# First layer's second and third set of modulations: from TensorE in the projections to POOL and one-column products in attention

## The chip, the cores and the metric

The kernel runs on one core of one Trainium2 chip. The metric is the device time of one execution in microseconds. The core has five engines that work side by side: TensorE (PE; its weight loads are listed as PEld), VectorE (DVE), ScalarE (ACT), POOL (GpSimd) and SyncE (SP), which here only issues DMAs. Each engine works through its own queue in order; semaphores make it wait for others.

## The reference, cut to what matters

Two layers over 1024 latent tokens and 256 context tokens of width 1024. Every layer is steered by six vectors ("modulations") for the latents and six for the context, each a product of an activated conditioning vector with a 1024 x 6144 matrix. The first layer's mixer is attention beside a convolution:

```python
sc = jax.nn.silu(c)
scc = jax.nn.silu(c_ctx)
for l in range(DEPTH):
    mod_l = jnp.split((sc @ ada_w[l] + ada_b[l])[:, None, :], 6, axis=-1)
    mod_c = jnp.split(scc @ ada_w[l] + ada_b[l], 6, axis=-1)
    h_lat = rms_norm(x, norm1_g[l]) * (1 + mod_l[1]) + mod_l[0]
    h_ctx = rms_norm(ctx, norm1_g[l]) * (1 + mod_c[1]) + mod_c[0]
    ...                                   # l == 0: even_mixer, attention | convolution
    x = x + mod_l[2] * y_lat
    h = rms_norm(x, norm2_g[l]) * (1 + mod_l[4]) + mod_l[3]
    x = x + mod_l[5] * conv_ffn(h, ...)
    ...                                   # the same for ctx with mod_c
```

So modulations 0 and 1 are needed before the first projections, and 2 to 5 only after the mixer.

## The kernel before

Activations lie with channels on partitions and tokens along the free dimension: 8 tiles of 128 x 1280, context first. All large products are made of three products of rounded parts (`mm3`, lines 336 to 340): a number is split into a high and a low part, and high x high, high x low and low x high are summed. Weights come in units of 128 x 1024 (`wunit`): SyncE loads them, ScalarE rounds the high part, POOL subtracts for the low part (line 332).

The order of each engine's instructions is set when the kernel is built: the program is traced in the order of the Python code, and a planner with its own estimate of times then orders each engine's queue, taking what is ready first and, among that, what was traced first. The context manager `later(400)` makes what is traced inside it count as traced 400 instructions later. Tiles with one `tag` share `bufs` buffers. A `Side` is a list of generators whose pieces of work are traced between the steps of the main work: `run(us)` adds to an account, and each piece takes from it what it yields.

The work around the change, all in the first layer (`layer0`):

- *Start.* The sums of squares of x, and the first set of modulations (`ada_set` for set 0; a set is two modulations, 2048 columns). `ada_gen` loads the weights in tiles, 128 rows by 512 or 1024 columns, and TensorE multiplies them, in plain float32: the 128 x 32 tile `sc` (both conditioning vectors and 30 columns of zeros) stands still and 512 columns of weights stream through (line 365, tile `adaps`). The trace shows each such product as two records. ScalarE copies the result, TensorE turns it (line 374, `adapt`), VectorE adds the bias into `modT` (line 379).
- *Projections.* Four channel blocks of the convolution's gated input (`l0_conv`: two dense products each, tiles `dc` and `dl`, then VectorE multiplies by ScalarE's sigmoid), and five blocks of queries, keys and values (`l0_block`: per 128 tokens a 128 x 256 result `qkv` or `qkl`; ScalarE squares and copies it into `z`, VectorE and POOL normalize and rotate it, SyncE stores it). Between them a `Side` traces the depthwise convolution with 31 taps (`conv_taps`): 22 taps (30 in the last block) are VectorE's multiply-adds (`self.stt`, line 1162), the other 8 are multiplied by ScalarE (line 692, tile `ctap`, three buffers) and summed by DMAs that POOL issues with accumulation (line 693). The weights of modulation sets 1 and 2 are loaded here too, in the three `ctap` buffers, with `later(400)`.
- *Attention* (`attention_all`). Four groups of three heads; units of 256 queries, 12 long ones over 1280 keys and 3 short ones over 256 context keys in each group. Steps of scores and of values are interleaved by due times: 9 steps for a long unit and 3 for a short one, 468 in all. TensorE makes scores `S`, VectorE the maximum (line 995), ScalarE the exponential (line 996), TensorE turns the result (line 1018, tile `pT`, tag `pt`, two buffers), ScalarE and VectorE split it into `ph` and `pl` (lines 1022, 1023), TensorE multiplies by the values (line 1029), and SyncE stores the output to DRAM tiles `od` (line 1041). After each step `side.run(0.14)` traces a piece of the preparation of the next group (`stack_gen`, tiles `zst` on POOL and ScalarE, turned by TensorE, line 963), and `more.run(0.22)` a piece of the convolution's layer norm (`l0_ln`) and then of `load_early`: finished chunks of the mixer's output are read back from `od` and split by POOL into two parts (lines 800 to 804).
- *Output projection.* Ten chunks of 128 channels, in the order 6, 7, 8, 9 (convolution), 0 to 5 (heads): seven were split during attention, the last three are loaded and split afterwards by ScalarE and VectorE (`load_split`, lines 502 and 503), beside the loads of x. Here modulation 2 is used first.

The sums of squares in `ss_finish` (line 418) are one-column products: a 128 x 128 block of squares stands still and one column of ones streams through, which sums over partitions.

## Time and profile before

| | |
|---|---|
| median of 3 runs | 3935.66 us (3933.4 to 3939.22) |
| profiled execution | 3939.62 us, span 3937.4 us |
| mean granted TensorE clock | 0.962 |
| busy share of the span | TensorE 92%, weight loads 74%, VectorE 55%, ScalarE 32%, POOL 34% |

The numbers of the trace below are times of one execution, counted from the first instruction. The rows that name a line, an engine and tiles give what the group wrote, an arrow, and what it read; `x128` is the number of records. A row of a stretch gives for each engine its busy time and the number of records, then the granted TensorE clock, the busy share of the 16 DMA engines and GB/s. A row of a wait gives who waited, for whom, the total in us, how often, and the longest. A row of the timeline gives start and length in us, and in brackets the idle time before it with what ended it.

### The profile page before, as it was taken

What the parts mean: (1) busy time and instruction counts of PE and PEld (TensorE: products, weight loads), DVE (VectorE), ACT (ScalarE), POOL (GpSimd) and SP (SyncE); (2) the same over time, 40 slices, a digit from 0 to 9 for tenths busy, and PEclk for the clock granted to TensorE, in tenths of its full rate; (3) what the DMA queues carried; (4) which work ended last, traced back from release to release, by engine and by line L of the source; (5) the groups of instructions that cost most, each with busy time, mean ns of one, the idle gap of its engine ahead of it and who ended that gap; (6) DMA issues with size and microseconds to landing.
All of it is one profiled execution on the core that took longest, in us unless ns stands there. A gap on an engine that the chain in (4) does not pass through costs nothing.

```text
span 3937.4 us, 47862 instructions
## 1 busy us (share of the span) xinstructions
PE 3610.4 (92%) x18784; PEld 2923.8 (74%) x18784; DVE 2173.8 (55%) x2720; ACT 1251.1 (32%) x2126; POOL 1328.3 (34%) x1003
## 2 busy tenths in 40 slices
PE   7987688888899999999999899999976899999998
PEld 4767567767785558888888788988765778888886
DVE  5976366667223235554554579645598554343435
ACT  4135566666232112222222332322211342222222
POOL 3258331100251112332221445445466652222123
PEclk9999789999999999999999999999988999999999
DMA  5476111000323331222111257622245421111111
GB/s 200 121 187 149 44 57 31 21 24 19 108 78 110 110 106 61 66 75 70 60 59 38 75 173 215 185 95 91 97 155 198 134 69 43 50 42 54 43 54 54
DMA packets 204016, 356.38 MB, mean 91 GB/s; under 512 B 23632, under 2 KB 124560, under 8 KB 203792
## 3 DMA queue, kind: packets, MB, share of 16 engines
q1 hardware_dynamic: 172240, 311.22, 24.2%
q0 software_dynamic: 27648, 35.76, 4.3%
q10 hardware_dynamic: 3904, 6.36, 0.5%
q8 instruction: 148, 2.42, 0.3%
q14 instruction: 76, 0.62, 0.0%
HBM read 275.04 MB, written 62.39 MB: 86 GB/s over the span
## 4 chain that ended last, share of the span: by engine, by line
PE 68%; DVE 11%; issue 4%; ACT 3%; DMA 2%; POOL 2%; SPq 0%; POOLq 0%; ACTq 0%; DVEq 0%
PE dl L338 13%; PE dl L339 13%; PE dl L340 13%; PE adaps L365 2%; PE pj L338 2%; PE pj L339 2%; PE pj L340 2%; PE pT L1018 2%; PE o L1029 2%; DVE nm L995 2%; DVE pl L1023 2%; PE dc L340 2%; PE dc L339 2%; PE dc L338 1%; PE S L978 1%
## 5 line engine op out<-in xcount | busy, mean ns | idle before, releaser
L332 POOL TENSOR_TENSOR wlo<-wraw,whi 128x1024 fp32r<-128x1024 f32 (+1 forms) x226 | 560.6, 2486 | 1366.5 <-ACT whi L331 1266.5
L339 PE MATMUL dl<-hl,whi 128*128 128x512 f32 x1920 | 764.5, 398 | 4.2 <-POOL hl L1158 2.8
L338 PE MATMUL dl<-hh,whi 128*128 128x512 f32 x1536 | 608.6, 397 | 5.1 <-ACT nt L456 3.2
L340 PE MATMUL dl<-hh,wlo 128*128 128x512 f32 x1536 | 609.3, 397 | 0.0
L331 ACT CAST whi<-wraw 128x1024 fp32r<-128x1024 f32 (+1 forms) x226 | 224.8, 1005 | 917.3 <-PE dl L339 421.2
L339 PEld LDWEIGHTS dl<-hl,whi 128*128 128x128 f32 x1920 | 362.7, 189 | 99.0 <-issue 11.7
L1067 DVE SCALAR_TENSOR_TENSOR fc<-dl,cols,fc 128x1023 f32<-128x1023 f32 x84 | 107.6, 1281 | 548.6 <-ACT fc L1066 548.6
L338 PEld LDWEIGHTS dl<-hh,whi 128*128 128x128 f32 x1536 | 289.2, 188 | 86.8 <-issue 14.2
L340 PEld LDWEIGHTS dl<-hh,wlo 128*128 128x128 f32 x1536 | 289.5, 188 | 77.5 <-issue 10.1
L842 DVE SCALAR_TENSOR_TENSOR x<-dl,modT,x 128x1024 f32<-128x1024 f32 x160 | 204.7, 1280 | 164.2 <-PE dl L340 162.7
L338 PE MATMUL dl<-gs,whi 128*128 128x512 f32 x640 | 252.9, 395 | 5.1 <-DVE fc L1069 5.1
L339 PE MATMUL dl<-gs,whi 128*128 128x512 f32 x640 | 251.6, 393 | 0.0
L340 PE MATMUL dl<-gs,wlo 128*128 128x512 f32 x640 | 250.5, 391 | 0.0
L1018 PE MATMUL pT<-ident,p 128*128 128x128 f32 x1008 | 170.0, 292 | 40.6 <-DVE pl L1023 33.7
L1023 DVE TENSOR_TENSOR pl<-pT,ph 128x512 fp32r<-128x512 f32 x252 | 167.6, 686 | 66.3 <-ACT ph L1022 65.6
L1022 ACT CAST ph<-pT 128x512 fp32r<-128x512 f32 x252 | 142.7, 587 | 157.6 <-PE pT L1018 156.3
L995 DVE TENSOR_REDUCE nm<-S 128x1 f32<-128x1280 f32 (+1 forms) x120 | 153.0, 1275 | 55.5 <-PE S L979 51.5
L1029 PE MATMUL o<-ph,vs 128*128 128x256 f32 x504 | 146.5, 304 | 34.4 <-ACT ph L1022 17.4
L1018 PEld LDWEIGHTS pT<-ident,p 128*128 128x128 f32 x1008 | 124.3, 149 | 63.2 <-DVE pl L1023 47.3
L1162 DVE SCALAR_TENSOR_TENSOR conv<-u,cols,conv 128x1287 f32<-128x1287 f32 (+14 forms) x96 | 160.8, 1705 | 0.9
L365 PE MATMUL adaps<-adaw,sc 128*32 128x512 f32 x384 | 150.3, 621 | 7.8 <-DMA adaw<-in_adaw 7.4
L338 PE MATMUL dl<-hl,whi 128*128 128x512 f32 x384 | 154.9, 405 | 1.4 <-ACT whi L331 0.8
(368 smaller groups left out, 8351.8 us busy)
## 6 DMA issues: line engine op xcount, KB each, us to landing
wraw<-in_wup SPq DMA_DIRECT2D x88, 512.0 KB, 3.5
adaw<-in_adaw SPq DMA_DIRECT2D x128, 256.0 KB, 2.6
wraw<-in_wdn SPq DMA_DIRECT2D x44, 512.0 KB, 3.5
adaw<-in_adaw SPq DMA_DIRECT2D x32, 512.0 KB, 4.4
df<-in_dftf POOLq DMA_DIRECT2D x64, 256.0 KB, 4.2
wraw<-in_w1f SPq DMA_DIRECT2D x24, 512.0 KB, 3.6
x<-in_xT SPq DMA_DIRECT2D x16, 640.0 KB, 9.3
spd<-so SPq DMA_DIRECT2D x68, 128.0 KB, 2.7
```

Source lines behind the costliest of these rows:

```text
L331: nc.scalar.copy(hi[:, :cols], raw[:, :cols])
L332: nc.gpsimd.tensor_tensor(out=lo[:, :cols], in0=raw[:, :cols], in1=hi[:, :cols].bitcast(F32), op=ALU.subtract)
L338: mm(out, lhsT=lh, rhs=rh, start=first, stop=False)
L339: mm(out, lhsT=lh, rhs=rl, start=False, stop=False)
L340: mm(out, lhsT=ll, rhs=rh, start=False, stop=last)
L365: nc.tensor.matmul(ps[32 * i:32 * i + 32, :], lhsT=self.sc[:, k, :], rhs=w[:, b:b + 512], start=(k == 0), stop=(k == KD - 1), tile_positio ...
L842: nc.vector.scalar_tensor_tensor(out=xl, in0=pl, scalar=self.mod(l, j, m, 0), in1=xl, op0=ALU.mult, op1=ALU.add)
L995: nc.vector.tensor_reduce(out=nm[:, i:i + 1], in_=s, op=ALU.max, axis=AX.X, negate=True)
L1018: nc.tensor.transpose(pt[:, (2 * a + i) * P:(2 * a + i + 1) * P], p[:, kc * P:(kc + 1) * P], self.ident)
L1023: nc.vector.tensor_tensor(out=pl, in0=pt, in1=ph.bitcast(F32), op=ALU.subtract)
L1029: nc.tensor.matmul(o, lhsT=vs[:, kc], rhs=x[:, a * 256:a * 256 + 256], start=(kc == 0 and j == 0), stop=(kc == nk // P - 1 and j == 1))
L1162: self.nc.vector.scalar_tensor_tensor(out=out, in0=a, scalar=s, in1=b, op0=ALU.mult, op1=op)
```

## The change

Modulation sets 1 and 2 of the first layer are no longer formed by `ada_set` in the projections. A new generator, `ada_vec`, forms them during attention, as a third list of side work (`slow`, `slow.run(0.25)` after each step, a piece of 1.4 for each weight tile). For each set and each quarter of 512 columns it loads 8 weight tiles of 128 x 512; for both conditioning vectors POOL multiplies the tile by that vector's column (one number per partition) and adds the product to an accumulator of 128 x 512. Then TensorE sums over the partitions with one-column products, four blocks for each vector, into a PSUM tile `adv` with the tag `pt`, and VectorE adds the bias. The buffers for this (two each for weights, accumulators and products, 2 KB per partition each) lie in attention's pool; for them the mixer's chunks that are split during attention are six instead of seven, and `load_split` brings four afterwards instead of three.

```diff
+    def ada_vec(self, l, s, cs, wbuf, acc, psf, pool=None):
+        nc = self.nc
+        bias = self.col(f"adab{l}", 48, 2)
+        for j in range(4):
+            a = [acc(i) for i in range(len(cs))]
+            for k in range(KD):
+                w = wbuf()
+                nc.sync.dma_start(out=w, in_=self.i["adaw"][l, s, k, j // 2][:, j % 2 * 512:j % 2 * 512 + 512])
+                for i, c in enumerate(cs):
+                    f = self.sc[:, k, c:c + 1]
+                    if k == 0 or pool:
+                        t = pool() if k else a[i]
+                        (nc.gpsimd if pool else nc.vector).tensor_scalar(out=t, in0=w, scalar1=f, scalar2=None, op0=ALU.mult)
+                        if k:
+                            self.add(a[i], a[i], t, pool=True)
+                    else:
+                        self.stt(a[i], w, f, a[i])
+                yield 0.7 * len(cs)
+            ps = psf("adv")
+            n = len(cs)
+            for b in range(4):
+                for i in range(n):
+                    nc.tensor.matmul(ps[:, b * n + i:b * n + i + 1], lhsT=a[i][:, b * P:(b + 1) * P],
+                                     rhs=self.ones[:, 0:1], start=True, stop=True)
+            m = slice(s * 16 + 4 * j, s * 16 + 4 * j + 4)
+            self.add(self.modT[l][:, m, cs[0]:cs[-1] + 1], ps[:, :4 * n].rearrange("p (b c) -> p b c", c=n),
+                     bias[:, m, cs[0]:cs[-1] + 1])
...
-            ada = [(0, 1), (0, 2)]
...
-                if ada and (blk, c) in self.ADA:
-                    with self.later(400):
-                        self.ada_set(*ada.pop(0), lambda: c2.tile([P, UL], F32, name="adaw", tag="ctap", bufs=3), self.a_ps)
...
-            hs = early + self.load_split(oh, [self.od[k] for k in order[7:]], T, (512, TC + 512, T), 2)
+            hs = early + self.load_split(oh, [self.od[k] for k in order[6:]], T, (512, TC + 512, T), 2)
...
-    ADA = ((None, 0), (None, 1))
...
+        slow = Side()
+        for n in (1, 2):
+            slow.add(self.ada_vec(0, n, (0, 1), lambda: ab.tile([P, 512], F32, name="adaw", tag="adaw", bufs=2),
+                                  lambda i: ab.tile([P, 512], F32, name="adacc", tag="adacc", bufs=2),
+                                  lambda name: self.pa.tile([P, 512], F32, name=name, tag="pt", bufs=self.npt),
+                                  lambda: ab.tile([P, 512], F32, name="adap", tag="adap", bufs=2)))
...
-                        early = self.two_parts(7, "oc", self.oc)
+                        early = self.two_parts(6, "oc", self.oc)
...
-                                                  for c in {3: (0,), 5: (1, 2), 7: ()}[g]]))
+                                                  for c in {3: (0,), 5: (1,), 7: ()}[g]]))
...
             more.run(self.MORE)
+            slow.run(self.SLOW)
         more.drain()
+        slow.drain()
...
-    LEAD, SIDE, MORE = 1.35, 0.14, 0.22
+    LEAD, SIDE, MORE, SLOW = 1.35, 0.14, 0.22, 0.25
```

## The prediction

> **What bounds the kernel now.** I read the page first, for the share of TensorE and for the rows of the products that the change removes; then busy time by stretch, for the two stages that it touches; then the waits, the timeline and single tiles inside them.
>
> ```profile
> span 3937.4 us, 47862 instructions
> PE 3610.4 (92%) x18784; PEld 2923.8 (74%) x18784; DVE 2173.8 (55%) x2720; ACT 1251.1 (32%) x2126; POOL 1328.3 (34%) x1003
> L365 PE MATMUL adaps<-adaw,sc 128*32 128x512 f32 x384 | 150.3, 621 | 7.8 <-DMA adaw<-in_adaw 7.4
> ```
>
> TensorE is busy for 92% of the span, so work taken from it counts unless another engine is as full in that stage. The 384 records are six sets (two records to a product); the change takes two of them, 128 records. They lie in the projections (94 to 387 us); attention runs from 420 to 1007.
>
> ```profile
> core 0: us, PE busy (x) PEld busy (x) DVE busy (x) ACT busy (x) POOL busy (x), PEclk, DMA share, GB/s
> 94.00:387.00 293.00, 267.97 (x1726) 221.11 (x1724) 233.24 (x315) 100.03 (x414) 149.18 (x113) 0.98 0.58 149
> 420.00:1007.00 587.00, 474.33 (x2968) 397.39 (x2968) 380.05 (x576) 361.69 (x661) 93.16 (x167) 0.92 0.10 30
> 753.80:877.40 123.60, 102.80 (x680) 87.14 (x680) 84.63 (x128) 77.04 (x147) 7.99 (x19) 0.97 0.06 17
> 893.30:1007.20 113.90, 91.60 (x598) 77.13 (x596) 79.02 (x120) 65.50 (x117) 0.00 (x0) 0.97 0.04 9
> ```
>
> The projections are bound by TensorE (268 of 293 us) with VectorE close behind (233). Attention is a tight loop through TensorE, ScalarE and VectorE, TensorE 81% busy, POOL only 16%. The last two rows are the same stretch of head group 2 and of group 3, from the first of 15 stores of head outputs to the last (11 long units, 3 short), as in the row
>
> ```profile
> 893.35 114.28 SPq L1041 DMA_DIRECT2D od<-ot  x15
> ```
>
> I use them below.
>
> **The change part by part.**
>
> *Products out of the projections.* Busy time of this tile alone in the stage, one block of the timeline, and the waits:
>
> ```profile
> 94.00:387.00 293.00, 36.62 (x128) 4.94 (x128) 1.13 (x2) 0.98 0.58 149
> ...
> 153.62 0.28 PE L339 MATMUL qkv<-wlo,hh 128*128 128x256 f32 x1
> 153.74 0.28 PE L340 MATMUL qkv<-whi,hl 128*128 128x256 f32 x1
> 153.94 1.05 PE L365 MATMUL adaps<-adaw,sc 128*32 128x512 f32 x4
> 154.93 0.38 PE L338 MATMUL qkv<-whi,hh 128*128 128x256 f32 x1
> 155.15 0.28 PE L339 MATMUL qkv<-wlo,hh 128*128 128x256 f32 x1
> ...
> DVE conv L1158 <- DMA acc<-ctap: 23.5, 3, 14.6
> PE qkl L338 <- ACT z L751: 10.8, 6, 2.7
> DVE modT L379 <- PE adapt L374: 8.3, 1, 8.3
> PE adaps L365 <- DMA adaw<-in_adaw: 7.4, 3, 5.0
> ```
>
> Four records take 153.74 to 155.15, where two of the steps before (0.12 us) would have stood: 1.17 us each, and 32 such blocks are 37.4 us. TensorE waited 7.4 us more for their weights. The eight turns (two sets of four) are within a microsecond or two and left out. So 45 us leave TensorE's queue: it had 268 - 37 = 231 busy, and 25 - 7 = 18 us of waits that stay, which makes the stage 249 us.
>
> The cover is then nearly gone: VectorE has 233 us of work in the stage (mostly the depthwise taps), and only 16 us of slack. Some of its waits go with the sets, though. It waited 8.3 us for the turned sums; and the weights sat in the three buffers of the taps that ScalarE forms for accumulating DMAs:
>
> ```profile
> L692 ACT ACTIVATE ctap<-u,cols x24: 1365/1374/1492, 182.7 to 368.9; 128x1280 f32<-128x1280 f32 x3, 128x1283 f32<-128x1283 f32 x3, 128x1286 f32<-128x1286 f32 x3, 128x1289 f32<-128x1289 f32 x3
> DMA to landing us min/median/max: 5.1/5.5/9.1
> ...
> L1162 DVE SCALAR_TENSOR_TENSOR conv<-u,cols,conv x96: 1537/1554/3691, 92.4 to 312.4; 128x1281 f32<-128x1281 f32 x8, 128x1282 f32<-128x1282 f32 x8, 128x1284 f32<-128x1284 f32 x8, 128x1285 f32<-128x1285 f32 x8
> L1162 DVE SCALAR_TENSOR_TENSOR conv<-u,cols,conv 128x1287 f32<-128x1287 f32 (+14 forms) x96 | 160.8, 1705 | 0.9
> ```
>
> The first ScalarE tap starts at 182.7, when the first set is through, although VectorE's own taps of the first convolution began at 92.4; the 24 taps then go one after the other, some 6.9 us each with ScalarE's 1.37, and VectorE waits 23.5 us for their sums. Without the sets this chain can start some 80 us earlier. I estimate a gain between 20 us (VectorE's queue holds TensorE back for more than half) and 55 us (the 18 us of left waits shrink too), and take 38: TensorE's 45 less a few, because VectorE stands at 94% of the new stage.
>
> *One-column products in attention.* 8 quarters of a set, each 8 products (4 blocks, 2 contexts): 64, at two records each. The nearest row is exactly this form, the sums of squares, run in attention:
>
> ```profile
> 433.45 0.35 PE L418 MATMUL sums<-ones,acc 128*128 128x1 f32 x2 [0.57 <-DVE pl L1023]
> 433.66 0.36 PE L418 MATMUL sums<-ones,sq 128*128 128x1 f32 x2
> ...
> 434.33 0.36 PE L1029 MATMUL o<-pl,vs 128*128 128x256 f32 x1
> ...
> L1022 ACT CAST ph<-pT 128x512 fp32r<-128x512 f32 x252 | 142.7, 587 | 157.6 <-PE pT L1018 156.3
> L1023 DVE TENSOR_TENSOR pl<-pT,ph x252: 671/682/693, 432.6 to 1004.3; 128x512 fp32r<-128x512 f32 x126
> ```
>
> The four pairs of records take 433.45 to 434.33, 0.88 us, so 64 take 14.1. How much of it shows? Between head groups 2 and 3 TensorE's work differs by 102.8 - 91.6 = 11.2 us and the stretch by 9.7: TensorE's work comes through at 0.87 to 1, in spite of 17 to 20% idle, since that idle is waiting for the loop itself. So +12 to +14. Beside that each burst holds one of the two `pt` slots until a VectorE add, and the next four turns must then share one slot. The slot's round there is the copy and the subtraction, 0.59 + 0.68 us (the last two rows), at worst 1.3 us in each of 8 bursts, 10 in all. I take half: +19 together, with ends +8 (the bursts fall into waits) and +30.
>
> *The multiplications on POOL.* The 64 weight tiles need 128 multiplications by a column and 112 additions, 128x512. The trace has the addition, but no multiplication by a column on POOL; copies bound it from below, the addition from above.
>
> ```profile
> L1158 POOL TENSOR_TENSOR ssacc<-ssacc,sq 128x512 f32<-128x512 f32 x48 | 64.3, 1340 | 20.3 <-ACT sq L405 14.0 <-issue 5.1
> L803 POOL CAST och<-ysrc 128x256 fp32r<-128x256 f32 x35 | 12.7, 399 | 110.3 <-DMA ysrc<-od 103.5 <-issue 6.8
> L944 POOL CAST vs<-p 128x640 fp32r<-128x640 f32 x3 | 2.2, 717 | 8.2 <-DMA p<-zd 8.2
> ```
>
> Copies go at (717 - 399) / 384 = 0.83 ns an element, so 0.61 us for 512. I take that, the nearer kind: 128 x 0.61 + 112 x 1.34 = 228 us; with 1.34 for the multiplication 322. POOL's 93 us in attention become 321 (55% of 587) or 415 (71%): it fits, and I price it at nothing, covered by POOL's idle time. If that cover fails, the second rival has the price. The Trainium skill ("GPSIMD Engine Reference", Performance versus the Vector engine) measures 769 ns for its best loop over 512 elements; by that, an estimate, POOL would need some 248 us, and the sum would be the same. No run here shows the multiplication.
>
> *Queues.* SyncE issues 64 loads of 256 KB in attention (DMA share 0.10 there) for 32 of 512 KB in the projections (0.58). With two buffers, a load waits until POOL is done with the tile two back, at most 3.9 us (two multiplications, two additions). Behind it on SyncE wait the stores of the head outputs and the loads of the next head group; the stores have two buffers and come 8 us apart on average (15 in 114 us), so nothing. On POOL the copies for the next head group now queue behind up to a 1.34 us addition; TensorE's turns wait for them. Three groups of ten tiles; mostly early, so I put it into the upper end of the +30.
>
> *One chunk less loaded early.* Six chunks of attention's output are split on POOL during attention (5 x 1.13 us less there), and four instead of three afterwards.
>
> ```profile
> 1007.72 1.04 SPq L781 DMA_DIRECT2D ysrc<-od  x2
> 1008.82 2.35 SPq L620 DMA_DIRECT2D x<-in_xT  x5
> 1011.90 0.88 SPq L781 DMA_DIRECT2D ysrc<-od  x1
> ...
> 1022.48 0.62 ACT L502 CAST yh<-ysrc 128x512 fp32r<-128x512 f32 x1 [10.55 <-DMA ysrc<-od]
> 1023.13 0.69 DVE L503 TENSOR_TENSOR yl<-ysrc,yh 128x512 fp32r<-128x512 f32 x1 [10.41 <-ACT yh L502]
> ...
> PE pj L338 <- ACT yh L502: 9.2, 1, 9.2
> ```
>
> The third chunk's load stands behind five loads of x, and TensorE waits 9.2 us for it. The fourth stands beside the third and adds its own cast and subtraction, 0.62 + 0.69 us, once or twice: +2, ends 0 and +5.
>
> **Sum.** -38 + 19 + 2 = -17 us against the profiled execution: span 3937.4 to 3920, its time 3939.6 to 3922.6. The median of the three runs, 3935.66, lies 4.0 below that execution, so I predict 3918.7.
>
> **Rivals.**
>
> *VectorE takes the place of TensorE.* With 233 us of taps and rotations in a stage of 249, any wait of VectorE comes through. Then the projections gain only 20 us, attention takes its 19, the chunk 2: 0 to -2, time 3935. For it: the 94%. Against it: in the first 90 us of the stage both were full (TensorE first, VectorE third) and TensorE did not wait; and 32 us of VectorE's 60 idle there end on what the change removes or starts earlier (8.3 + 23.5).
>
> ```profile
> 94.00:144.00 50.00, 50.00 (x264) 43.18 (x262) 49.61 (x32) 6.43 (x7) 14.74 (x4) 1.00 0.12 36
> 144.00:185.00 41.00, 41.00 (x238) 24.48 (x237) 40.93 (x28) 4.32 (x10) 2.93 (x2) 1.00 0.65 202
> ```
>
> *POOL makes TensorE wait (slower).* The products stand in TensorE's queue in a fixed order; if the last addition of a quarter isn't done, attention stops. POOL's queue also holds the next group's copies, which themselves wait for TensorE. What such a wait costs elsewhere (the longest of the kernel, last figure):
>
> ```profile
> PE sums L418 <- POOL ssacc L1158: 6.4, 2, 4.5
> ```
>
> At 4.5 us for each of 8 bursts it is +36, net +19: 3954.7. It decides from (17 + 8) / 8 = 3.1 us a burst. For it: the multiplication's unknown price. Against it: POOL at 55%, with one quarter (30 us of POOL) due every 56 us: the program hands out 64 tiles over 358 of attention's 468 steps, at 587 / 468 = 1.25 us a step.
>
> *POOL locks VectorE out.* Taps with two inputs in SBUF take 1.54 to 3.69 us while POOL splits weights, so a neighbour's POOL work can cost VectorE. Attention's subtraction never varies, 671 to 693 ns with POOL busy or idle. If the 252 of them lost the 0.15 us by which the taps' mean lies above their median (1.705 against 1.554), it would be +38, about as slow as the rival before. The Trainium skill ("SBUF — State Buffer", SBUF: two separate sides) says that the shared port is an exclusive lock between POOL and VectorE operations with two SBUF inputs or in a two-port mode; the subtraction reads PSUM and one SBUF tile, so by that rule it is free, and the trace agrees (671 to 693).
>
> *Attention hides the bursts.* Half of the products fall into the loop's waits and the projections give 45: -45 + 8 + 2 = -35, 3900.
>
> **How the numbers follow.** 0.2% is 7.9 us; I count less than that as no change. The forecast (-8 to -28) 0.48; bursts hidden 0.16; VectorE instead of TensorE 0.20; POOL late 0.12; VectorE locked out 0.04. Faster 0.64, same 0.20, slower 0.16. The forecast's own range is 3908 to 3928; the range for 8 in 10 reaches to -42 (gain 52, cost 10) and to +12 (gain 20, cost 32): 3894 to 3948.
>
> **What would show it.** In the profile after: no 128x512 `adaps` products before 400 us; ScalarE's taps starting near 95 us; blocks of projections ending near 349 instead of 387; VectorE above 90% there. In attention: 128 records `adv` of 128x1, in 8 bursts of 1.8 us; POOL above 50%; TensorE's waits for POOL near nothing; the last store 575 to 590 us after the first reduction (420 to 1007 before). The wait before the first output product of chunk columns near 10 us. It is wrong if the projections end less than 20 us earlier, or if waits of `adv` for POOL exceed 3 us a burst.

## The result and the profile after

The changed kernel takes 3981.12 us (median of 4 runs, 3978.85 to 3997.11) against 3934.53 for the kernel before, run beside it: a ratio of 1.0127, 95% interval 1.0098 to 1.0155. It is 47 us slower where I had forecast 17 faster; the profiled executions differ by 41.4. The first lines of the page of the changed kernel, then busy time of its two stages (projections, attention), in the columns of the rows by stretch in the prediction:

```profile
span 3979.1 us, 48225 instructions
PE 3593.6 (90%) x18776; PEld 2940.8 (74%) x18776; DVE 2166.2 (54%) x2723; ACT 1251.1 (31%) x2125; POOL 1678.5 (42%) x1233
...
94.00:361.00 267.00, 230.45 (x1587) 216.18 (x1587) 226.57 (x306) 93.00 (x398) 161.70 (x113) 0.95 0.46 106
387.00:1037.00 650.00, 504.71 (x3136) 426.34 (x3134) 382.19 (x588) 365.54 (x676) 423.93 (x414) 0.90 0.16 52
```

TensorE is busy for 17 us less over the span and the span is 41.7 us longer, so the time went into waits. By stage, in the profiled execution of each kernel (points read from the timelines):

| us | before | after | difference |
|---|---|---|---|
| last q/k product of the projections | 384.0 | 361.3 | -22.7 |
| from there to the first store of a head output | 72.3 | 74.3 | +2.0 |
| attention: first to last of its 60 stores | 550.9 | 602.0 | +51.1 |
| output projection: last store to the first FFN product | 159.5 | 167.3 | +7.8 |
| the rest | 2770.7 | 2774.2 | +3.5 |

The sum is +41.7, the difference of the spans. The new instructions, as groups of the changed kernel (busy time, mean ns of one, idle time before them):

```profile
L395 POOL TENSOR_SCALAR adap<-adaw,sc 128x512 f32<-128x512 f32 x112 | 175.0, 1576 | 12.6 <-DMA adaw<-in_adaw 12.4
L1191 POOL TENSOR_TENSOR adacc<-adacc,adap 128x512 f32<-128x512 f32 x112 | 141.9, 1287 | 0.0
L395 POOL TENSOR_SCALAR adacc<-adaw,sc 128x512 f32<-128x512 f32 x16 | 24.9, 1570 | 4.9 <-PE adv L405 4.4 <-PE zT L996 0.4
L405 PE MATMUL adv<-ones,adacc 128*128 128x1 f32 x128 | 20.4, 281 | 18.7 <-POOL adacc L1191 18.7
```

A multiplication by a column takes POOL 1.57 us, above both ends that I had worked with (0.61 and 1.34). The first late burst, in TensorE's timeline, with ScalarE's row beside it and a burst 188 us later; then the rows by stretch for the two bursts, with the granted clock behind the busy times:

```profile
560.94 0.59 PE L405 MATMUL adv<-ones,adacc 128*128 128x1 f32 x2 [7.61 <-POOL adacc L1191]
561.38 1.09 PE L1051 MATMUL pT<-ident,p 128*128 128x128 f32 x4
562.84 3.15 PE L405 MATMUL adv<-ones,adacc 128*128 128x1 f32 x14 [0.36 <-POOL adacc L1191]
562.30 0.47 ACT L1029 ACTIVATE p<-S,nm 128x256 f32<-128x256 f32 x1 [9.77 <-PE pT L1051]
748.73 1.64 PE L405 MATMUL adv<-ones,adacc 128*128 128x1 f32 x14
...
560.90:566.20 5.30, 4.90 (x21) 4.50 (x22) 1.28 (x3) 1.61 (x5) 5.30 (x6) 0.50 0.43 120
748.70:750.40 1.70, 1.70 (x17) 1.70 (x16) 1.29 (x2) 0.59 (x1) 1.70 (x2) 0.98 0.00 0
```

TensorE stands for 7.6 us before a product whose sum POOL has not finished, and ScalarE for 9.8 us, since the transposes `pT` come behind the product. The last 14 records of the burst (7 products, two records each) then take 3.15 us, at a granted clock of 0.50. In the later burst, before which TensorE had worked for 3.7 us without a break, they take 1.64 us at 0.98.

In the projections ScalarE's taps start at 89 us, as I had said, and this is what follows (group of the tile, then waits between 94 and 361 us, TensorE's last):

```profile
L717 ACT ACTIVATE ctap<-u,cols x24: 1352/1374/1384, 89.3 to 247.3; 128x1280 f32<-128x1280 f32 x3, 128x1283 f32<-128x1283 f32 x3, 128x1286 f32<-128x1286 f32 x3, 128x1289 f32<-128x1289 f32 x3
ACT ctap L717 <- DMA acc<-ctap: 96.6, 21, 12.4
POOL acc L718 <- DMA acc<-ctap: 74.2, 18, 8.4
...
PE qkl L338 <- ACT z L776: 10.9, 6, 5.8
PE qkv L338 <- ACT whi L331: 7.6, 1, 7.6
PE qkv L339 <- POOL wlo L332: 7.0, 3, 3.2
PE qkv L338 <- ACT z L776: 6.0, 2, 4.8
```

ScalarE waits 96.6 us there for accumulating DMAs, and POOL 74.2 (45.5 and 38.1 in the kernel before). Both also make TensorE's weights (`whi`, `wlo`), and ScalarE copies its results (`z`). With two smaller rows (2.6 and 2.4 us, both for ScalarE's `z`) TensorE's waits come to 36.5 us: all of them are for ScalarE or POOL, none for VectorE.

### The profile page after: what moved, and what is told of

It reads as the page before. It is cut to its first block, busy times and chain, and to the rows that moved or that the text cites. A ratio compares the mean times of both kernels' runs of the same rounds, so it can differ in the third digit from the quotient of the medians.

```text
span 3979.1 us, 48225 instructions
## 1 busy us (share of the span) xinstructions
PE 3593.6 (90%) x18776; PEld 2940.8 (74%) x18776; DVE 2166.2 (54%) x2723; ACT 1251.1 (31%) x2125; POOL 1678.5 (42%) x1233
## 4 chain that ended last, share of the span: by engine, by line
PE 65%; DVE 8%; issue 4%; DMA 2%; POOL 2%; ACT 2%; SPq 0%; POOLq 0%; DVEq 0%; ACTq 0%
PE dl L338 13%; PE dl L339 13%; PE dl L340 13%; PE adaps L365 2%; PE pj L338 2%; PE pj L340 2%; PE pj L339 2%; PE dc L340 2%; PE dc L338 2%; PE dc L339 2%; PE Bp L1568 1%; PE pT L1051 1%; PE U L1555 1%; DVE nm L1028 1%; PE o L1062 1%
## 5 line engine op out<-in xcount | busy, mean ns | idle before, releaser
L332 POOL TENSOR_TENSOR wlo<-wraw,whi 128x1024 fp32r<-128x1024 f32 (+1 forms) x226 | 575.9, 2554 | 1290.9 <-ACT whi L331 1204.2
L339 PE MATMUL dl<-hl,whi 128*128 128x512 f32 x1920 | 763.7, 398 | 3.8 <-POOL hl L1191 3.3
L339 PEld LDWEIGHTS dl<-hl,whi 128*128 128x128 f32 x1920 | 362.2, 189 | 98.8 <-issue 12.6
L338 PEld LDWEIGHTS dl<-hh,whi 128*128 128x128 f32 x1536 | 289.1, 188 | 85.7 <-issue 11.7
L340 PEld LDWEIGHTS dl<-hh,wlo 128*128 128x128 f32 x1536 | 289.1, 188 | 79.6 <-issue 11.7
L395 POOL TENSOR_SCALAR adap<-adaw,sc 128x512 f32<-128x512 f32 x112 | 175.0, 1576 | 12.6 <-DMA adaw<-in_adaw 12.4
L1029 ACT ACTIVATE p<-S,nm 128x1280 f32<-128x1280 f32 (+1 forms) x120 | 139.2, 1160 | 61.5 <-DVE nm L1028 32.9
L1062 PE MATMUL o<-pl,vs 128*128 128x256 f32 x504 | 152.4, 325 | 4.4 <-DVE pl L1056 4.1
```

The costliest lines, as they stand in the source:

```text
L332: nc.gpsimd.tensor_tensor(out=lo[:, :cols], in0=raw[:, :cols], in1=hi[:, :cols].bitcast(F32), op=ALU.subtract)
L338: mm(out, lhsT=lh, rhs=rh, start=first, stop=False)
L339: mm(out, lhsT=lh, rhs=rl, start=False, stop=False)
L340: mm(out, lhsT=ll, rhs=rh, start=False, stop=last)
L395: (nc.gpsimd if pool else nc.vector).tensor_scalar(out=t, in0=w, scalar1=f, scalar2=None, op0=ALU.mult)
L1062: nc.tensor.matmul(o, lhsT=vs[:, kc], rhs=x[:, a * 256:a * 256 + 256], start=(kc == 0 and j == 0), stop=(kc == nk // P - 1 and j == 1))
```

## The experiments

All stages in one table, in us: the end of the projections; from the first turned input of attention to its first score; attention's stores; output projection as above; the median; and the ratio to the kernel before, run beside it, with its 95% interval. The stages are those of one profiled execution of each kernel.

| kernel | proj. end | first score | attention | output | time | ratio |
|---|---|---|---|---|---|---|
| before | 384.0 | 10.0 | 550.9 | 159.5 | 3934.5 | |
| after | 361.3 | 16.8 | 602.0 | 167.3 | 3981.1 | 1.0127 (1.0098 to 1.0155) |
| drop_sets | 360.2 | 10.0 | 548.4 | 158.1 | 3906.5 | 0.9925 (0.9909 to 0.9941) |
| six_chunks | 382.4 | 9.9 | 547.4 | 167.7 | 3938.0 | 1.0012 (1.0001 to 1.0022) |
| no_products | 358.8 | 17.1 | 556.6 | 168.0 | 3937.2 | 1.0000 (0.9990 to 1.0010) |
| no_pool | 358.7 | 10.1 | 558.4 | 167.3 | 3933.3 | 0.9992 (0.9980 to 1.0003) |
| slow20 | 361.9 | 17.1 | 585.4 | 167.1 | 3962.0 | 1.0066 (1.0050 to 1.0083) |
| bcast | 358.6 | 14.9 | 572.3 | 167.1 | 3946.1 | 1.0031 (1.0021 to 1.0041) |
| late_products | 361.7 | 14.3 | 557.5 | 225.5 | 3992.6 | 1.0148 (1.0131 to 1.0166) |
| pipe_after | 359.2 | 14.6 | 595.0 | 167.8 | 3972.2 | 1.0094 (1.0080 to 1.0108) |
| pipe_slow21 | 360.1 | 14.6 | 552.9 | 167.1 | 3926.2 | 0.9978 (0.9969 to 0.9988) |
| pipe_no_heads | 357.2 | 14.4 | 579.6 | 176.7 | 3969.7 | 1.0099 (1.0083 to 1.0116) |
| taps_dve | 389.5 | 10.0 | 544.7 | 157.4 | 3935.7 | 1.0004 (0.9994 to 1.0014) |
| taps_gap | 385.2 | 9.9 | 545.4 | 157.4 | 3937.8 | 1.0006 (0.9993 to 1.0019) |
| two_acc | 353.2 | 10.0 | 552.6 | 157.1 | 3902.0 | 0.9913 (0.9896 to 0.9930) |
| before_two_acc | 372.4 | 11.7 | 545.9 | 159.3 | 3929.3 | 0.9985 (0.9974 to 0.9995) |
| best6 | 349.4 | 14.9 | 576.6 | 167.5 | 3944.8 | 1.0028 (1.0014 to 1.0041) |
| best_late | 347.5 | 12.8 | 560.4 | 207.6 | 3969.9 | 1.0091 (1.0073 to 1.0109) |
| pipe_best | 354.4 | 12.6 | 559.0 | 167.3 | 3924.8 | 0.9980 (0.9971 to 0.9989) |
| pipe_final | 348.7 | 12.6 | 558.7 | 168.7 | 3921.0 | 0.9963 (0.9949 to 0.9976) |

Where attention is not touched its stage still varies between 545 and 553 us, so differences of a few us there say nothing.

**The parts one by one.** First the removal alone, on the kernel before:

```diff
-            ada = [(0, 1), (0, 2)]
+            ada = []                       # and modT starts at zero
```

> The kernel before without the first layer's modulation sets 1 and 2: they are not computed at all (modT starts at zero), seven chunks stay early, attention is untouched. It is the worth of the removal alone. If the 45 us that leave TensorE's queue are limited by the taps that ScalarE forms (its queue waits for accumulating DMAs, 96.6 us in the changed kernel), the last q/k product ends near 361 us as in the changed kernel, and the total is 3934.5 - 21 = 3913. If something that the change does elsewhere (the moved chunk, its memory) costs in the projections, they end near 349 as I forecast, and the total is 3897.

Measured: the projections end at 360.2, 24 us sooner, as in the changed kernel. What the change adds elsewhere costs nothing there; the gain itself is smaller than the 38 that I forecast. The total, 3906.5, lies between the two that I had named.

One chunk less, on the kernel before:

```diff
-            ... self.load_split(oh, [self.od[k] for k in order[7:]], ...
+            ... self.load_split(oh, [self.od[k] for k in order[6:]], ...
...
-                        early = self.two_parts(7, "oc", self.oc)
+                        early = self.two_parts(6, "oc", self.oc)
...
-                                                  for c in {3: (0,), 5: (1, 2), 7: ()}[g]]))
+                                                  for c in {3: (0,), 5: (1,), 7: ()}[g]]))
```

> The kernel before with only six chunks loaded early instead of seven; nothing else changes. In the changed kernel the output projection's products end 159 us after the last store as before, but the FFN's first product comes at 167.3 instead of 159.5, since the first normalized inputs (hh) are made at 156 us instead of at 108. If the chunk does that (its memory is what hh needs), this kernel is 7 to 9 us slower, 3942 to 3943, with hh at 156. If modulation set 2 from attention does it, it is within 3 us of before and hh stays at 108.

The output projection grows by 8.2 us and the kernel by 0.12%. In ScalarE's timeline the first of the normalized inputs, before and with six chunks (the last stores at 1007.2 and 999.8 us):

```profile
1114.76 0.51 ACT L460 ACTIVATE hh<-nt,modT 128x256 fp32r<-128x256 f32 x1 [6.56 <-DVE nt L452]
...
1156.13 0.51 ACT L460 ACTIVATE hh<-nt,modT 128x256 fp32r<-128x256 f32 x1 [0.58 <-PE pj L340]
```

They come 108 us and 156 us after the last store. So the FFN starts late because its inputs now wait for the last products of the output projection, and the chunk alone does it. That `hh` needs memory which the chunks or their loads hold would explain it; only the timing is shown.

Then POOL's work without the products, and the products without POOL's work, on the changed kernel:

```diff
-            ps = psf("adv")
-            ...                            # 64 products, VectorE's addition
+            for i, c in enumerate(cs):
+                self.add(self.modT[l][:, m, c], a[i][:, 0:4], bias[:, m, c], pool=True)
```

> The changed kernel with all of its loads, multiplications and additions on POOL, but without the 64 one-column products and without a slot of pt: POOL itself writes modT from four columns of the accumulator (so the modulations are not the reference's). Theory 1, late accumulators: POOL's work alone costs nothing, the loss is the products' slot of pt waiting for POOL; attention's stores then span 551 to 556 us (602 in the changed kernel, 551 before), total 3981 - 48 = 3933. Theory 2, the bursts cost of themselves: the same. Theory 3, POOL's load delays the copies for the next head group or the loads on SyncE's queue: attention stays at 580 or more, total above 3960.

```diff
-            a = [acc(i) for i in range(len(cs))]
+            a = self.fix                   # two tiles, set to zero once
             for k in range(KD):
-                ...                        # load, multiplications, additions
                 yield 0.7 * len(cs)
```

> The changed kernel with the 64 products, their slot of pt and VectorE's additions at the same steps, but without the weight loads, the multiplications and the additions on POOL: the products read two constant tiles (so the modulations are only the bias). Theory 1, late accumulators: what is left is TensorE's own 14 us and a part of the shared slot, attention 563 to 570 us, total 3943 to 3950. Theory 2, the bursts cost of themselves: attention stays at 590 or more, total above 3968. Theory 3: attention near 551 + 19 as by theory 1, so the run before tells these two apart.

POOL's work alone brings attention to 556.6 us, the products alone to 558.4 (less than the 563 to 570 that I expected), both together to 602.0. Against 547.4 (six chunks, neither) that is 9 and 11, not far above the spread of the stage, and together 55: the loss is the meeting of the two. POOL's work also delays the first score by 7 us, with or without the products:

```profile
375.45 3.10 POOL L395 TENSOR_SCALAR adap<-adaw,sc 128x512 f32<-128x512 f32 x2
378.50 0.63 POOL L984 CAST zst<-zl 128x192 fp32r<-128x192 f32 x2
...
383.67 1.05 PE L996 MATMUL zT<-identr,zst 128*128 128x128 f32 x4 [9.37 <-POOL zst L987]
```

This is the changed kernel at the start of attention: POOL multiplies from 372 us on, the copies `zst` that TensorE turns come behind, and TensorE stands for 9.4 us (2.3 at this point in the kernel before).

**Is it lateness?** A cheaper multiplication, and a slower pace:

```diff
-                        (nc.gpsimd if pool else nc.vector).tensor_scalar(out=t, in0=w, scalar1=f, ...)
+                        self.add(t, w, f.to_broadcast([P, 512]), ALU.mult, pool=True)
```

> The changed kernel with the multiplication written as a product of two tensors, the second the column spread over 512 elements, instead of tensor times one number per partition. If POOL's price is that of any operation with two tensor inputs (1.28 us, the additions' median), POOL has 128 x 0.29 = 37 us less, a quarter falls from 43 to 38 us, and by theory 1 attention falls from 602 to 570 to 592. If the spread column costs as the column did (1.57), nothing changes; if more, attention grows past 602, which theory 1 also says and the rival (a fixed price for each burst) does not.

```profile
L1191 POOL TENSOR_TENSOR adap<-adaw,sc 128x512 f32<-128x512 f32 x112 | 114.7, 1039 | 6.5 <-DMA adaw<-in_adaw 6.5
```

As a product of two tensors the same multiplication takes 1.04 us: POOL has 128 x 0.53 = 68 us less, and attention falls by 30. POOL's price is a cause.

```diff
-    LEAD, SIDE, MORE, SLOW = 1.35, 0.14, 0.22, 0.25
+    LEAD, SIDE, MORE, SLOW = 1.35, 0.14, 0.22, 0.20
```

> The changed kernel with weight tiles handed out at 0.20 a step instead of 0.25: a tile every 7 steps instead of 5.6, a quarter every 56 steps (66 to 70 us) instead of 45 (53 to 56 us), the last at step 448 of 468. POOL needs 16 x 1.57 + 14 x 1.28 = 43 us for a quarter and some 12 us for its other work. Theory 1 (POOL is late at the products, and the transposes that need the same slots wait for it): POOL keeps up, TensorE's waits for the accumulators go from 18.7 us to under 5, attention falls from 602 to 563 to 575, total 3942 to 3955. Rival (each burst costs 6 us wherever it stands, since it takes a slot of pt): attention stays at 595 or more, total 3975 or more.

585.4, between the two theories: pace helps, but the products still stand one tile behind the last addition, and one burst waits 10.4 us for its sums.

So the products were moved away from the additions (with `adacc` in four buffers and `adap` in one):

```diff
+            yield 11.2
             ps = psf("adv")
```

> The changed kernel with the products of each quarter a whole quarter later (45 steps) than its last tile, with four accumulators instead of two and one product buffer instead of two (additions and multiplications stand in one queue, so the second buffer does nothing). POOL's work and its price stay: 345 us. Theory 1 (POOL late at the products): its lag of some 10 us is inside the 53 us of delay, TensorE's waits for the accumulators go to 0, attention falls from 602 to 560 to 570, total 3939 to 3951. Rival (a burst costs 6 us whenever it stands, since it takes a slot of pt): 595 or more. If POOL is not only late but behind by more than a quarter, the later bursts still wait, and attention ends between.

Attention takes 557.5, and TensorE's waits for the sums inside it are gone. But the generator hands out no tile during its delay, which I had overlooked: two of the eight quarters end behind attention, where they cost 58 us, and POOL's load is thinned: from 700 to 900 us it is busy for 51 to 56 us of 100, where it is busy for 86 to 89 in the changed kernel. So the run does not tell the delay from the thinner load. In the next, with the same buffers, the tiles go on, and the products of each quarter are kept in a list (`pend`) and traced later:

```diff
+                if k == 4 and self.pend:
+                    self.pend.pop()()      # products of the quarter before
```

> The changed kernel in which the products of a quarter are traced after the fifth tile of the next quarter (28 steps, some 35 us later) while the tiles go on without a stop; four accumulators, one product buffer; the last quarter's products 22 steps after its last tile. POOL's multiplications stay as they are (1.57 us). Theory 1 (only the lateness costs): no wait of the products for POOL, attention 557 to 568 us instead of 602, output projection 167 as before, total 3938 to 3950. Rival (POOL saturated, at 92 of 100 us, its lag grows past 35 us, or the stop of the tiles was what helped): attention 580 or more, total 3960 or more.

595.0: a miss, and as the rival had it. POOL is behind by more than the 35 us of delay. What put it behind stands in SyncE's rows (stores of head outputs, loads of chunks) and POOL's:

```profile
545.90 11.67 SPq L1083 DMA_DIRECT2D od<-ot  x3
557.68 1.01 SPq L833 DMA_DIRECT2D ysrc<-od  x2
...
561.05 1.78 POOL L836 CAST och<-ysrc 128x256 fp32r<-128x256 f32 x5 [11.04 <-DMA ysrc<-od]
```

POOL's next instruction is a copy of a chunk; its load stands on SyncE's queue behind three stores that wait for attention itself; POOL, in order, does no multiplication meanwhile. The second quarter's sums were done at 530.8 us, the third quarter's only at 640.7. Between 750 and 850 us it is busy for 91 us of 100, and it does not catch up. Two runs tell pace from chunk copies:

```diff
-    LEAD, SIDE, MORE, SLOW = 1.35, 0.14, 0.22, 0.25
+    LEAD, SIDE, MORE, SLOW = 1.35, 0.14, 0.22, 0.21
```

> pipe_after with tiles handed out at 0.21 a step: a quarter every 53 steps (62 to 65 us), its products some 42 us after its last tile, the last at step 454. POOL has 8 us more for each quarter. If the missing slack keeps POOL late, it catches up after the third quarter, most bursts find their sums ready and attention falls from 595 to 560 to 575, total 3938 to 3952. If lateness is not what costs (the rival with a fixed price for each burst), attention stays at 590 or more.

```diff
-                        early = self.two_parts(6, "oc", self.oc)
+                        early = self.two_parts(4, "oc", self.oc)
...
-                                                  for c in {3: (0,), 5: (1,), 7: ()}[g]]))
+                                                  for c in {3: (), 5: (), 7: ()}[g]]))
```

> pipe_after without the two chunks of head outputs that POOL splits during attention (only the four of the convolution stay early); they are loaded after it, which makes the output projection longer by some 5 to 15 us. If the chunk copies that wait for loads behind the stores put POOL behind, attention falls from 595 to 565 to 580, and POOL's waits for the loads of chunks fall from 28.8 to under 15 us. If the four chunks of the convolution do that already, or the price of the multiplication alone, attention stays at 585 or more.

With the pace, all of POOL's work at 1.57 us and all 64 products, attention takes 552.9 us, less than the 560 to 575 that I expected; the products wait for POOL no more (0.6 us in all, for VectorE):

```profile
L409 PE MATMUL adv<-ones,adacc 128*128 128x1 f32 x128 | 14.8, 246 | 0.6 <-DVE pl L1065 0.6
```

The same 100 us in the changed kernel, then in this one:

```profile
550.00:650.00 100.00, 69.07 (x402) 58.92 (x401) 48.41 (x76) 42.12 (x80) 90.51 (x91) 0.81 0.22 70
...
550.00:650.00 100.00, 82.49 (x559) 70.27 (x558) 68.89 (x104) 61.56 (x117) 71.43 (x80) 0.98 0.19 59
```

POOL 71 instead of 91, TensorE 559 records instead of 402, the clock 0.98 instead of 0.81. Counted store by store from the first, the changed kernel falls behind this one by 11.5 us between its stores at 547 and 572 us, and by 17.8 between those at 613 and 642. These two stretches hold the bursts at 561 and 627 us, the two before which TensorE is listed as waiting for sums; they make 29 of the 49 us. The other 20 lie in smaller steps, which were not traced one by one.

Without the head chunks' copies attention falls from 595.0 to 579.6, inside what I expected if they put POOL behind: a part, some 15 us. POOL's waits for the loads of chunks fall from 28.8 to 11.2 us, as expected; but pipe_slow21 has 29.7 us of them and no late sum, so by themselves they cost nothing where POOL has slack. Lateness of POOL's sums is shown as the cause.

**The projections.** Which of two theories limits the gain, the chain of accumulating DMAs or VectorE, was tried on drop_sets:

```diff
-    PTAPS = (8, 8, 8, 0)
+    PTAPS = (0, 8, 8, 0)
```

> As drop_sets (no modulation sets 1 and 2), and the first convolution's eight taps of ScalarE and the accumulating DMAs go to VectorE. drop_sets ended its projections at 360. Theory T (the chain of accumulating DMAs, one after the other, holds ScalarE's and POOL's queues, and so TensorE's weights and the q/k copies): a third of the chain is gone, TensorE's 34 us of waits fall by 8 to 12, projections end at 348 to 354. Theory V (VectorE is the bound, 242 of 296 us busy): VectorE gets 8 x 1.55 = 12 us more and the projections end at 366 to 372.

Both missed: 389.5. POOL's and VectorE's rows show a third thing:

```profile
152.98 37.48 POOL L333 TENSOR_TENSOR wlo<-wraw,whi 128x1024 fp32r<-128x1024 f32 x1 [1.08 <-ACT whi L332]
...
151.45 36.81 DVE L1163 SCALAR_TENSOR_TENSOR conv<-u,cols,conv 128x1285 f32<-128x1285 f32 x25
...
198.41 1.36 ACT L693 ACTIVATE ctap<-u,cols 128x1283 f32<-128x1283 f32 x1 [39.77 <-DMA acc<-ctap]
...
200.09 0.58 PE L339 MATMUL qkv<-whi,hh 128*128 128x256 f32 x1 [35.73 <-ACT z L745]
```

A subtraction that takes 2.6 us elsewhere takes 37.5, until 2.2 us after 25 taps of VectorE that follow each other without a seam. POOL's next accumulating DMA stands behind it, ScalarE's next tap waits 39.8 us for that DMA, ScalarE's copy of TensorE's result stands behind the tap, and TensorE waits 35.7 us: this is how the chain on the two queues reaches TensorE. With maxima between the taps:

```diff
+                if c < 3 and j % 6 == 5:
+                    nc.vector.tensor_reduce(out=g, in_=acc[:, TC + GAP:], op=ALU.max, axis=AX.X)
```

> As taps_dve, with one more VectorE operation after every sixth tap: a maximum over the 1024 last columns of the sum just written (one input; its result is not used). In taps_dve the subtraction wlo on POOL, 2.6 us elsewhere, took 37.48 us from 152.98 on, and ended 2.2 us after 25 VectorE taps without a break (151.45 to 188.26). Theory L (taps with two inputs in SBUF lock POOL out as long as they follow each other): POOL gets in during a maximum, the longest wlo falls under 13 us, and the projections end earlier than the 389.5 of taps_dve, at 360 to 375, though VectorE has some 15 operations of 1.1 us more. Rival (POOL waited for something that the trace does not show, such as the DMA queue): wlo stays at 30 us or more and the projections end at 389.5 + 16 = 405.

The longest subtraction falls to 9.9 us, as theory L has it, and the projections end at 385.2, not at 360 to 375. Nor did POOL get in during a maximum: it ended at 161.7, 2.2 us after a seam between two taps (159.50 to 159.53), the first maximum came at 163.1, and the tap behind that seam took 3.5 us instead of 1.55. In drop_sets it is the same: the subtraction from 125.20 to 135.63 ended 2.2 us after the last of VectorE's taps in a row (133.38, then a product that reads PSUM). That taps lock POOL out is thus seen in three traces; the inserted maxima did not prove it. The longest subtraction of the projections takes 10.2 us in the changed kernel and 9.4 in pipe_final, so the lock is there too, and it is not what two accumulators change.

Two accumulators, on drop_sets and on the kernel before:

```diff
-            acc2 = pool.tile([P, UL], F32, name="acc2", tag="acc2", bufs=1)
+            acc2 = [pool.tile([P, UL], F32, name=f"acc2{i}", tag=f"acc2{i}", bufs=1) for i in range(2)]
...
-                t = pool.tile([P, UL], F32, name="ctap", tag="ctap", bufs=3)
+                t = pool.tile([P, UL], F32, name="ctap", tag="ctap", bufs=2)
...
-                nc.gpsimd.dma_start(out=acc2[:, a:b], in_=t[:, a:b], accum_op=ALU.add)
+                nc.gpsimd.dma_start(out=acc2[pt.index(j) % 2][:, a:b], in_=t[:, a:b], accum_op=ALU.add)
...
```

> As drop_sets, with the accumulating DMAs of a convolution going in turn to two accumulators instead of one, with two buffers for the taps instead of three (the memory does not hold more), and one more VectorE addition for each of three convolutions (4 us). Theory T: two DMAs fly at a time, the chain of 24 shortens from 157 us (89 to 246) to 90 to 120 us, ScalarE's waits for it fall from 95 to under 60 us, projections end at 345 to 355 instead of 360. Theory V: VectorE has 4 us more, projections end at 360 to 364.

```profile
L694 ACT ACTIVATE ctap<-u,cols x24: 1353/1374/1383, 88.2 to 228.8; 128x1280 f32<-128x1280 f32 x3, 128x1283 f32<-128x1283 f32 x3, 128x1286 f32<-128x1286 f32 x3, 128x1289 f32<-128x1289 f32 x3
ACT ctap L694 <- DMA acc<-ctap: 57.8, 20, 9.1
```

ScalarE's waits fall from 94.7 (drop_sets) to 57.8 us, the projections end 7 us sooner; the chain shortens less than I expected, from 157 to 141 us. In the table, the ten kernels without the sets in the projections and with one accumulator end them at 357.2 to 361.9 us (taps_dve and taps_gap apart), the five with two at 347.5 to 354.4: the gain is clear of the spread.

> The kernel before with the two accumulators and two tap buffers alone; the sets stay on TensorE in the projections, their weights in the tap buffers, now two. If the gain of two_acc belongs to the taps' chain whatever else stands there, the projections end 5 to 8 us earlier (376 to 379), total 3927 to 3930. If the two buffers slow the weights of the sets (each pair of tiles waits for TensorE), they end later than 384 and it is no gain: 3935 to 3945. In the kernel before the chain lay behind the sets and TensorE was full, so I hold the second for likelier.

A miss by the second reading, which I held for likelier: the kernel before gains 11.6 us in its projections and 0.15% in all. The repair is worth as much without the change.

**Versions.** best6 is bcast with 0.20 a step and two accumulators; best_late is bcast with the stopping delay and two accumulators; pipe_best is pipe_after with the cheaper multiplication, two accumulators and the tiles starting 12 steps later; pipe_final is pipe_slow21 with the cheaper multiplication and two accumulators.

> A version to beat the changed kernel and perhaps the one before: multiplication as product of two tensors (1.04 us instead of 1.57, attention 572 instead of 602), tiles handed out at 0.20 a step, and two accumulators for the accumulating DMAs with two tap buffers (projections end at 353 instead of 360). By theory 1 POOL needs 35 us of a quarter's 66, so attention falls to 558 to 566; with 7 us from the projections the total is 3925 to 3935. If pace and price do not add up (the bursts have a fixed price), attention stays at 570 and the total at 3939.

> As the run before, but in place of the slower pace the products come a quarter later, with four accumulators (0.25 a step; the last burst at step 403). By theory 1 no wait for POOL is left and attention is what no_pool has for the bursts (558.4) plus what POOL's work alone costs (no_products 556.6 against 547.4): 558 to 567, total 3923 to 3933.

> As the run before, with the multiplication as product of two tensors (1.04 us), two accumulators for the accumulating DMAs (projections end at 348 to 353), and the tiles starting 12 steps later, so that POOL copies the first head group's inputs first. Sum against the kernel before: projections -31 to -36, first score 10 us after the first turn (17 in the changed kernel), attention +8 to +14, output projection +8. Total 3915 to 3930. If what POOL's work costs in attention (9 us with 1.57) does not shrink with the cheaper multiplication, the upper end.

> pipe_slow21 with the cheaper multiplication (1.04 us) and two accumulators and two tap buffers for the accumulating DMAs. If the taps' chain limits the projections here too, they end at 347 to 354 instead of 360; with the cheaper multiplication the first score comes up to 4 us sooner; attention stays at 550 to 556 (no wait is left that a cheaper multiplication could shorten). Total 3912 to 3922. If the two theories do not add up, 3926.

best6 missed in attention (576.6): without the delay one burst, at 581 us, still waits for its sums. best_late had the tail of late_products. pipe_best and pipe_final took the times expected; pipe_final, at 3921.0, is 0.37% faster than the kernel before and 60 us faster than the changed kernel. The two accumulators alone give the kernel before 0.15% of that, so some 8 us (3929.3 against 3921.0) are left for the change itself. Its attention, 558.7, lies 3 us above what I expected and gained nothing visible from the cheaper multiplication: no product was late in pipe_slow21 either, and the profiled execution (3929.6 us) was the slowest of the seven.

## Why the prediction was wrong

*Projections, -38: measured -22.7.* TensorE's busy time came out as worked out (231; 230.45 in the row). The step that failed is that 18 us of waits stay: 267 - 230.45 = 36.6 us are left. I had counted the earlier start of the taps as a gain for VectorE only. The chain stands on ScalarE's and POOL's queues, and it now runs while these make TensorE's weights; before, it ran later (from 183 us on), and TensorE had the sets' products to do (144 to 274 us). With two accumulators the projections end at 347.5 to 353.2, near my 349 (the run with tiles 12 steps later: 354.4). So the number was that of the first rival (gain 20), but not for its reason: none of TensorE's 36.5 us of waits in the stage is for VectorE, which was busy for 85% of it (226.57 of 267), not above 90%.

*One-column products, +19.* They cost less when they are on time: attention 552.9 with them (pipe_slow21) against 550.9 before, and 558.4 with them alone (no_pool) against 547.4 with six chunks. That is 2 to 11 us, in a stage that varies by 8. The 14.1 us of TensorE's work was right (14.8 in the row of pipe_slow21); a part of it falls into the loop's waits, as in the fourth rival.

*Multiplications on POOL, priced at nothing: the step that turned the sign.* The price was outside the bounds, 1.57 us against 0.61 to 1.34, since neither a copy nor an addition is this operation. That alone was not it. POOL's share of attention was 424 of 650 us, 65%, between the 55 and 71% that I called a fit, and pipe_slow21 has the same work without a loss, at 72% (432.8 of 600 us). What I took for cover was an average. What decides is whether the sums of a quarter are there when the products' turn comes, and they had one tile's time, 7 us. The second rival had this mechanism, with 3.1 us a burst as the point from which it decides. Its price was too low: 4.5 us for each of 8 bursts, where 51.1 - 2 (the products on time) over 8 is 6.1, as a wait also empties the loop and lowers the clock. Nor did the loss come evenly: the bursts at 561 and 627 us took 29 us of it. And 4.5 was not the longest wait of TensorE for POOL in the trace before, as I wrote: at the start of attention it waited 13.3 us for `zst`. I gave the rival 0.12; the row "TensorE's waits for POOL near nothing" came out at 18.7 us, and the waits named for POOL are little more than a third of the loss, since what stands behind the products is listed under other names (ScalarE's 9.8 us for `pT` above is one).

*Queues.* "SyncE: nothing" failed: chunk loads behind the stores stopped POOL for up to 11 us in pipe_after, and for up to 7.3 (18.5 in all) in the changed kernel. The copies for the head groups, which I had put into an upper end, came 7 us later before the first score; of that 2 us are left at the first store of a head output.

*One chunk, +2: measured +7.8.* TensorE's wait for the loaded chunks was about as forecast (8.1 us; near 10). I priced the load and not what else waits at the end of that stage: the FFN's first inputs.

*POOL locks VectorE out.* Rightly dismissed for attention: the subtraction takes 671 to 694 ns in the changed kernel too.

```profile
L1056 DVE TENSOR_TENSOR pl<-pT,ph x252: 671/690/694, 417.1 to 1034.7; 128x512 fp32r<-128x512 f32 x126
```

The lock worked the other way, in the projections, where the taps have two inputs in SBUF.

## What to carry to other kernels

When work moves to an idle engine, compare its finish of each portion with the moment at which the next engine's queue reaches it, not its share of the stage. A product placed in an in-order queue right behind slow side work stops everything behind it, so place it a portion later and hand the work out at a pace that leaves slack for what else that queue waits for. And ask what the removed work had been covering: here it had kept TensorE full while ScalarE and POOL waited for DMAs.

## What the runs showed of the hardware

On POOL, a 128 x 512 multiplication by one number per partition takes 1.57 us, the same as a product with the column spread over 512 elements 1.04 us, and an addition of two full tiles 1.28 us. The Trainium skill ("GPSIMD Engine Reference", 3.1 Elementwise) gives 769 ns as the best case for 512 elements; the three times here are 2.0, 1.4 and 1.7 times that.

VectorE's operations with two SBUF inputs, one behind the other, kept POOL from a subtraction for 37.48 us; POOL came in at a seam of 0.03 us, and the next tap then took 3.5 us instead of 1.55. The Trainium skill ("SBUF — State Buffer", Who interferes with whom) says that a VectorE instruction with two SBUF inputs contends with a POOL instruction that reads SBUF, and that the shared ports are an exclusive lock; the traces agree, and add that a row of such instructions can hold it from end to end.

Accumulating DMAs into one 128 x 1280 tile went one at a time: in drop_sets the 24 taps started 6.8 us apart (157 us from the first to the last), and each DMA landed 5.3 us (median) after its issue.

A wait of TensorE costs more than its length: after 7.6 us of standing, 7 one-column products (14 records) took 3.15 us at a granted clock of 0.50, where after 3.7 us of unbroken work they took 1.64 us at 0.98.
